# Queueing the HGRN scores and outputs between the k tiles of the projections, and the activation sums in four steps

## The chip, the core and the metric

The kernel runs on one core of one Trainium2 chip. TensorE multiplies matrices, VectorE and ScalarE do elementwise work (ScalarE also the functions: Sigmoid, Exp, Ln, Square), GpSimd (POOL) does small elementwise work and issues some DMAs, SyncE (SP) issues most of the weight DMAs. Each engine executes its own queue strictly in order; semaphores tie the queues together. The metric is the device time of one execution in microseconds (us). The kernel before takes 1414.12 us, the median of three runs (1412.45 to 1414.85).

## The reference: what is computed

One block of a network over 256 tokens of width 2048, all in float32. The projection `z = rms_norm(x) @ w_in` has eight parts, and two branches work on them:

```python
hq, hf, hi, hg, aq, ak, av, gates = jnp.split(z, SPLIT_POINTS, axis=-1)   # z = u @ w_in
g = lb + (1.0 - lb) * sigmoid(hf)          # forget gate;  log_g = log(g), kk = 1 - g
q = silu(hq) * HG_DK ** -0.5
o = hgrn2_scan(q, kk, hi, log_g)           # 8 heads of 128; S_t = diag(g_t) S_{t-1} + k_t v_t^T, o_t = S_t^T q_t
y_a = rms_norm(o, hg_norm_w) * silu(hg)
y_b = chunk_band_attention(aq, ak, av)     # 16 heads of 64, relative-position bias
merged = sigmoid(ga) * (y_a @ w_branch_a) + sigmoid(gb) * (y_b @ w_branch_b)
h = x + merged @ w_out
h = h + square(relu(rms_norm(h) @ w_up)) @ w_down
return rms_norm(h, norm_final_w)
```

The recurrence (HGRN) is what the change is about. It equals a masked product: `scores[t, s] = sum_k q[t, k] * exp(b[t, k] - b[s, k]) * kk[s, k]` for `s <= t`, where `b` is the running sum of `log_g`, and `o = scores @ v`. The factor depends on `t`, `s` and `k` together, so the kernel builds it from blocks of 2, 8, 32 and 128 tokens, within each of which the exponent splits into a factor for `q` and one for `kk`.

## The kernel before

**Products in three parts.** Every float32 product of a projection is made from a high and a low part of each operand. Two helpers load weights and make the parts: ScalarE casts the raw tile to the high part `wh_...` (line 89) and VectorE subtracts it from the raw tile for the low part `wl_...` (line 90). The raw tiles have six buffers, `wh` and `wl` four each; every such tile is 128 x 1024. This work is issued under a high priority, so that the scheduler puts it as early in each engine's order as the buffers permit. The activations `xT`, `ya`, `yb`, `mT`, `hT`, `uT` are kept transposed, also as high and low part.

**Two forms of a projection.** `gemm` (lines 154 to 158) makes 512 output columns for all 256 tokens: 16 k tiles, for each two halves `m` of the tokens, for each `mm3` with three products of 128x512 (lines 143 to 145), 96 products in all. `gemm_t` (lines 160 to 174) makes 256 transposed columns: for each of 16 k tiles and two column blocks one product of 128x512 and one of 128x256 (lines 170, 171), 64 products in all. Its two halves are added by `add_parts` (lines 178 and 179): ScalarE copies one half out of PSUM, VectorE adds the other. Both take one of the two buffers of the pool `ps_acc`; transposes take one of two in `ps_tp`, scores `ps` and outputs `po` one of two in `ps_sm`. A buffer is free when its last reader has read it.

**The order of the work.** Python emits the instructions in program order. A scheduler then orders them by priority, which follows program order outside the blocks of high priority, and a model of when each is ready; the result is one fixed queue for each engine. Nothing is chosen while it runs: an instruction that waits holds up all that stand behind it on its engine. ScalarE changes between the tables of its functions by a table load, which is an instruction of its own.

**The HGRN stage.** The eight heads are worked on as four pairs 0 to 3, in two groups of two pairs. `fq(u)` makes the inputs of a pair: the projections `hf` and `hq` (those of pairs 0 and 1 at the head of the kernel), then `hf_pair` (lines 298 to 310: `f`, `kk`, `lg` with an Ln, `b` by a scan) and `hq_pair` (lines 316 to 324: `sq` with a Sigmoid, then `q`). `v_chunk(g)` makes the values `v` of a group from `acc_hi`, `hg_chunk(g)` its output gate `gw` from `acc_hg`.

`hgrn_scores(n, ...)` (lines 348 to 425) makes the scores `sd` and `so` of a pair, all at once: first the diagonal and the tokens next to it (`ps{n}_1h`, line 355: 4 products of 128x192), then for each block size B of 2, 8 and 32 the factors (`el`, `kl`, `er`, `rr`, `qr`: VectorE differences and products, ScalarE Exp; lines 361 to 388) and the products `ps{n}_Bh` (line 395, 4 of 128x192), whose results VectorE writes into `sd` under masks, and last the block of 128 tokens (`c128`, `kc`, `ql`, lines 404 to 417, two products of 128x128, a copy to `so`). That makes 16 products of 128x192 and 2 of 128x128 for a pair. These products are plain float32, and the profile records each as two passes (its x8 are four products).

`hgrn_out(g, h0, ...)` (lines 428 to 461) makes the outputs of a pair for each half `m` of the tokens: `po` (lines 439 and 440; 4 + 2 products of 128x128), its squares `osq` on ScalarE (line 444), their sum `os` on VectorE, `rsqrt` (lines 95 and 96: VectorE `ms`, then a power `ro` on GpSimd) and `o` on VectorE (line 450). It returns a function that transposes `o` into `tpo` (line 458, two transposes for each `m`) and splits it into `ya` (ScalarE cast, VectorE subtraction). `hgrn_group` (line 476) calls this for both pairs of a group and then both of the transposing functions. The calls stand at lines 483 to 496:

```python
vs0 = v_chunk(0)
gws0 = hg_chunk(0)
s0 = hgrn_scores(0, *a0)
a2 = fq(2)
s1 = hgrn_scores(1, *a1)
a3 = fq(3)
hgrn_group(0, s0, s1, vs0, gws0)
```

and likewise for group 1, with the first attention projection `acc_q0` (`aq00`) before `hgrn_group(1, ...)`. The second one, `aq01`, is made in the attention stage, by `qk_chunk`, which reads `aq00` out with `add_parts` first. The next are `ak00` and `ak01`.

**After it.** The attention follows, then the gate projections, the merge (`ba`, `bb`), the output projection `wo` and the MLP (`up`, `dn`). The gates, `wo`, `up` and `dn` run as `Unit`s with a Strassen-like scheme on blocks of 2 x 2: seven products in place of eight, for which `combos` (lines 588 to 613) makes four sums S5, S4, S2 and S7 of blocks of the activations, each split into high and low part (a ScalarE cast, a VectorE subtraction of 128x512), from four block sums `a00` to `a11` (VectorE). The unit uses them in the order S5, S4, S2, S7. `combos` is called for `x` (before the gates), for the merged `m` (line 904, in the merge at `n == 2`), for `h` and for each quarter of `u`. `wo` runs as the units `wo0` and `wo2`, and the sums of `h` are made within `wo2`. For the last two it is the last entry of a unit's list of steps. A step carries a key, and `Unit.plain(n, ks)` issues, before its own products, all steps whose key is at most `ks[-1] // 4`, since these have to come before the k tile that it reads; `step` issues one step at each of the places between the unit's parts.

Of the kernel before, what the change touches and what calls it, by code (L numbers as in the profile page):

```python
# [16 lines left out]
P = 128  # L17
# [33 lines left out]
def tile_hybrid_block(  # L51
# [97 lines left out]

    def gemm(lhs, w, n0, nkt, what, wide=False):  # L150

        acc = new_acc(what)
        for kt, wh, wl in weights(w, n0, nkt, NC, what, wide=wide):
            for m in range(NM):
                mm3(acc[:, m, :], *lhs_of(lhs, kt, m), wh, wl, kt == 0, kt == nkt - 1)
        return acc

    def gemm_t(rhs, w, n0, nkt, what):

        acc = new_acc(what)  # L160
        for a in weights(w, n0, nkt, T, what):
            mm_t(acc, rhs, nkt, *a)
        return acc
# [184 lines left out]
    def hgrn_scores(n, kk, b, q):  # L348

        sd = hp.tile([P, 2, NM, P], F32, name=f"sd{n}", tag="sd", bufs=2)  # L350

        for h in range(2):
            ps = ps_sm.tile([P, NM, 192], F32, name=f"ps{n}_1{h}", tag="sm")
            for m in range(NM):
                nc.tensor.matmul(ps[:, m, :], kk[:, h, m * P:(m + 1) * P], q[:, h, m, :], start=True, stop=True)
            nc.vector.tensor_tensor(sd[:, h], ps[:, :, 0:P], bc(ident, 1, NM), op=ALU.mult)
            nc.vector.copy_predicated(sd[:, h].rearrange("p m (j u) -> p m j u", u=2)[:, :, :, 1],
                                      bc(mask1.bitcast(I32), 1, NM), ps[:, :, P:])

        for i, B in enumerate(LEVELS):  # L360
# [7 lines left out]
            kl = hp.tile([P, npar, 4, B], F32, name=f"kl{n}_{B}", tag="kl", bufs=3)  # L368
            nc.vector.tensor_tensor(kl, blocks(kk), el, op=ALU.mult)
# [7 lines left out]
            else:  # L377
# [4 lines left out]
                nc.vector.tensor_copy(rr, er[:, :, :, B - 1])  # L382
            qr = hp.tile([P, npar, 6, B], F32, name=f"qr{n}_{B}", tag="qr", bufs=2)
# [4 lines left out]
            nc.vector.tensor_tensor(qr[:, :, 5, :], qr[:, :, 4, :], bc(rr[:, :, 1], 2, B), op=ALU.mult)  # L388
            klf = kl.rearrange("p n v b -> p (n v b)")
# [14 lines left out]
        heads = lambda a: a.rearrange("p (h m) v b -> p h m v b", m=NM)  # L404
        r = rr.rearrange("p (h m) v -> p h m v", m=NM)
        r0, r1 = r[:, :, 0, :], r[:, :, 1, :]
        d128 = small.tile([P, 2, 4], F32, name=f"d128{n}", tag="d128", bufs=2)
        nc.vector.tensor_copy(c128[:, :, 2], r0[:, :, 3])
        nc.vector.tensor_tensor(c128[:, :, 1], r0[:, :, 2], r0[:, :, 3], op=ALU.mult)
        nc.vector.tensor_tensor(c128[:, :, 0], c128[:, :, 1], r0[:, :, 1], op=ALU.mult)  # L410
        nc.vector.tensor_copy(d128[:, :, 1], r1[:, :, 0])
        nc.vector.tensor_tensor(d128[:, :, 2], r1[:, :, 0], r1[:, :, 1], op=ALU.mult)
        nc.vector.tensor_tensor(d128[:, :, 3], d128[:, :, 2], r1[:, :, 2], op=ALU.mult)
        kc = hp.tile([P, 2, 4, 32], F32, name=f"kc{n}", tag="kc", bufs=1)
        nc.vector.tensor_tensor(kc, heads(kl)[:, :, 0], bc(c128, 3, 32), op=ALU.mult)
        ql = hp.tile([P, 2, 4, 32], F32, name=f"ql{n}", tag="ql", bufs=1)
        nc.vector.tensor_tensor(ql[:, :, 0, :], q[:, :, 1, 0:32], heads(er)[:, :, 1, 0, :], op=ALU.mult)
        nc.vector.tensor_tensor(ql[:, :, 1:4, :], heads(qr)[:, :, 1, 0:3, :], bc(d128[:, :, 1:4], 3, 32), op=ALU.mult)
# [461 lines left out]
    flush()  # L880


    mT = []

    def turned(lhs, n, name, src):

# [189 lines left out]
```

## Time and profile before

| | |
|---|---|
| median of three runs | 1414.12 us (1412.45 to 1414.85) |
| the profiled execution, its own time | 1415.3 us |
| its span | 1413.3 us |
| granted TensorE clock, mean | 0.996 |
| from the span's start to the first product of `acc_hi` | 54.9 us, TensorE busy 51.5 |
| HGRN stage, to the first product of `acc_ak` | 192.7 us, TensorE busy 187.5 |
| attention and first gates, 247.6 to 420 | 172.4 us, TensorE busy 172.3 |
| gates, merge and `wo`, 420 to 720 | 300.0 us, TensorE busy 296.9 |
| MLP, 720 to 1413.3 | 693.3 us, TensorE busy 682.0 |

In the rows of the profile, PE is TensorE, PEld its loading of weights, DVE VectorE, ACT ScalarE and POOL GpSimd; L143 is line 143 of the kernel. A group's row has line, engine, operation, result and operands, shape and count, then the busy time with the mean duration of one in ns, or least, mean and largest duration. A row of one instruction has its start and its duration in us. A row of a window of time has for each engine the busy time and, after x, the number of instructions, then the granted clock as a share of full speed, the DMA engines' busy share and the rate. A row of waits has the waiting instruction, an arrow to the instruction whose end released it, and the time that the engine stood idle, the number of such waits and the longest; the same arrow in square brackets behind a row gives the idle time ahead of that instruction. Products on TensorE overlap, and their ends are modelled, so that a duration is longer than the time from one start to the next.

### The profile page before, as it was taken

To read this page: it belongs to the slowest core of one execution; us is meant where nothing else is said; L and a number is where in the kernel's file an instruction comes from. 1 tells how busy PE (TensorE), PEld (TensorE's weight loads), DVE (VectorE), ACT (ScalarE), POOL (GpSimd) and SP (SyncE) were. 2 spreads that over 40 slices of the span, in tenths; PEclk is the share of its full clock that TensorE was granted. 3 is DMA by queue.
4 is the path that set the end of the run, shared out by engine and by line. 5 is a ranking of instruction groups with operands and counts; after the bars stand their busy time and mean duration, and the time that the engine had idled before them with its cause. 6 is when DMAs were issued, how large, how long until landed. Compare 5 with 4: busy or idle time off the path is not lost.

```text
span 1413.3 us, 18578 instructions
## 1 busy us (share of the span) xinstructions
PE 1390.2 (98%) x6562; PEld 1149.1 (81%) x6562; DVE 1120.0 (79%) x1410; ACT 912.6 (65%) x1173; POOL 138.6 (10%) x220
## 2 busy tenths in 40 slices
PE   9999999999999999999999999999999999999997
PEld 7888788878787888888877888888888888888885
DVE  7779887775658875687998878789777897878885
ACT  6766744464556665446767876677666876668764
POOL 3000101010000000001210001100101001110200
PEclk9999999999999999999999999999999999999999
DMA  9664444555568987558898899998899888998883
GB/s 318 234 195 148 135 158 135 184 173 167 183 223 256 263 235 256 185 177 258 249 282 252 245 269 243 278 280 245 259 292 283 254 229 250 289 293 263 258 255 115
DMA packets 122925, 327.42 MB, mean 232 GB/s; under 512 B 10944, under 2 KB 11712, under 8 KB 122448
## 3 DMA queue, kind: packets, MB, share of 16 engines
q1 hardware_dynamic: 103264, 264.80, 54.6%
q0 software_dynamic: 18416, 59.84, 21.3%
q10 hardware_dynamic: 1152, 1.60, 0.3%
q8 instruction: 51, 0.84, 0.2%
q14 instruction: 42, 0.34, 0.1%
HBM read 271.67 MB, written 10.49 MB: 200 GB/s over the span
## 4 chain that ended last, share of the span: by engine, by line
PE 89%; DVE 4%; DMA 2%; ACT 2%; issue 1%; POOL 0%; SPq 0%; POOLq 0%; ACTq 0%; DVEq 0%
PE acc_ak L171 2%; PE acc_aq L171 2%; PE acc_hf L171 1%; PE ps L395 1%; PE acc_hq L171 1%; PE tp_u L106 1%; PE acc_ga L144 1%; PE acc_ga L145 1%; PE acc_bb L143 1%; PE acc_ba L145 1%; PE acc_ga L143 1%; PE acc_av L143 1%; PE acc_bb L145 1%; PE acc_ba L143 1%; PE acc_ba L144 1%
## 5 line engine op out<-in xcount | busy, mean ns | idle before, releaser
L171 PE MATMUL acc_hf<-act_x,wh_hf 128*128 128x512 f32 x128 | 47.5, 408 | 1.7 <-DVE f L179 1.7
L171 PE MATMUL acc_aq<-act_x,wh_aq 128*128 128x512 f32 x128 | 47.8, 408 | 0.0
L171 PE MATMUL acc_hq<-act_x,wh_hq 128*128 128x512 f32 x128 | 45.9, 398 | 0.0
L171 PE MATMUL acc_ak<-act_x,wh_ak 128*128 128x512 f32 x128 | 44.8, 396 | 0.0
L170 PE MATMUL acc_aq<-act_x,wl_aq 128*128 128x256 f32 x120 | 35.2, 293 | 0.0
L90 DVE TENSOR_TENSOR wl_ga<-raw_ga,wh_ga 128x1024 fp32r<-128x1024 f32 x16 | 19.6, 1226 | 19.6 <-ACT wh_ga L89 19.6
L170 PE MATMUL acc_hf<-act_x,wl_hf 128*128 128x256 f32 x120 | 34.2, 285 | 0.0
L170 PE MATMUL acc_hq<-act_x,wl_hq 128*128 128x256 f32 x120 | 33.6, 280 | 0.0
L90 DVE TENSOR_TENSOR wl_av<-raw_av,wh_av 128x1024 fp32r<-128x1024 f32 x16 | 19.6, 1224 | 17.6 <-ACT wh_av L89 17.6
L170 PE MATMUL acc_ak<-act_x,wl_ak 128*128 128x256 f32 x120 | 33.5, 279 | 0.0
L89 ACT CAST wh_bb<-raw_bb 128x1024 fp32r<-128x1024 f32 x16 | 16.9, 1055 | 23.2 <-PE acc_ba L145 19.4
L90 DVE TENSOR_TENSOR wl_bb<-raw_bb,wh_bb 128x1024 fp32r<-128x1024 f32 x16 | 19.6, 1224 | 14.8 <-ACT wh_bb L89 14.8
L89 ACT CAST wh_av<-raw_av 128x1024 fp32r<-128x1024 f32 x16 | 16.9, 1053 | 22.0 <-PE acc_av L145 12.4
L89 ACT CAST wh_ba<-raw_ba 128x1024 fp32r<-128x1024 f32 x16 | 16.9, 1053 | 21.2 <-PE acc_bb L145 13.8
L89 ACT CAST wh_aq<-raw_aq 128x1024 fp32r<-128x1024 f32 x16 | 16.8, 1049 | 20.9 <-PE acc_aq L171 8.8
L90 DVE TENSOR_TENSOR wl_ba<-raw_ba,wh_ba 128x1024 fp32r<-128x1024 f32 x16 | 19.6, 1224 | 12.9 <-ACT wh_ba L89 12.9
L171 PEld LDWEIGHTS acc_hf<-act_x,wh_hf 128*128 128x128 f32 x128 | 24.2, 189 | 6.8 <-DVE f L179 2.0
L90 DVE TENSOR_TENSOR wl_aq<-raw_aq,wh_aq 128x1024 fp32r<-128x1024 f32 x16 | 19.6, 1224 | 12.5 <-ACT wh_aq L89 12.2
L171 PEld LDWEIGHTS acc_hq<-act_x,wh_hq 128*128 128x128 f32 x128 | 24.1, 188 | 5.6
L171 PEld LDWEIGHTS acc_aq<-act_x,wh_aq 128*128 128x128 f32 x128 | 24.2, 189 | 5.1 <-issue 0.7
L171 PEld LDWEIGHTS acc_ak<-act_x,wh_ak 128*128 128x128 f32 x128 | 23.9, 188 | 5.4
L89 ACT CAST wh_ga<-raw_ga 128x1024 fp32r<-128x1024 f32 x16 | 16.8, 1051 | 17.7 <-PE acc_ga L145 10.9
(1808 smaller groups left out, 5257.2 us busy)
## 6 DMA issues: line engine op xcount, KB each, us to landing
raw_hi<-in_w_in_n_dram SPq DMA_DIRECT2D x16, 512.0 KB, 4.2
raw_hg<-in_w_in_n_dram SPq DMA_DIRECT2D x16, 512.0 KB, 3.7
raw_aq<-in_w_in_t_dram SPq DMA_DIRECT2D x16, 512.0 KB, 4.3
raw_ak<-in_w_in_t_dram SPq DMA_DIRECT2D x16, 512.0 KB, 3.9
raw_av<-in_w_in_n_dram SPq DMA_DIRECT2D x16, 512.0 KB, 3.9
raw_ga<-in_w_in_t_dram SPq DMA_DIRECT2D x16, 512.0 KB, 4.6
raw_ba<-in_w_branch_a_dram SPq DMA_DIRECT2D x16, 512.0 KB, 4.5
raw_bb<-in_w_branch_b_dram SPq DMA_DIRECT2D x16, 512.0 KB, 4.6
```

Source lines behind the costliest of these rows:

```text
L89: (copy or nc.scalar.copy)(hi, src)
L90: nc.vector.tensor_tensor(lo, src, hi.bitcast(F32), op=ALU.subtract)
L106: nc.tensor.transpose(tp[:, j, :], src[:, j * P:(j + 1) * P], ident)
L143: nc.tensor.matmul(acc, hi, wh, start=first, stop=False, skip_group_check=True)
L144: nc.tensor.matmul(acc, hi, wl, start=False, stop=False, skip_group_check=True)
L145: nc.tensor.matmul(acc, lo, wh, start=False, stop=last, skip_group_check=True)
L170: nc.tensor.matmul(acc[:, cb, 0:T], wl[:, c], r[:, 0, :], start=False, stop=False)
L171: nc.tensor.matmul(acc[:, cb, :], wh[:, c], r.rearrange("p u t -> p (u t)"), start=kt == 0, stop=kt == nkt - 1)
L395: nc.tensor.matmul(ps[:, m, :], klf[:, a * P:(a + 1) * P], qrf[:, a * 192:(a + 1) * 192], start=True, stop=True)
```

## The change

A list `behind` holds pairs of a number and a function. `later` adds to its end; `tick(n)` subtracts n from the first number and, as long as the first number is at or below zero, takes the entry off and calls its function. `gemm` calls `tick(2)` ahead of the products of each k tile, `gemm_t` `tick(1)`. Numbers are not carried over: each entry counts from the moment at which it stands first.

`hgrn_scores` no longer emits its work but returns five steps: diagonal and factors of level 2; products of level 2 and factors of level 8; products of 8 and factors of 32; products of 32 and factors of 128; products of 128. Within the factors, `kl` now comes after `er` and `rr`, and `so` is allocated at the start. `scores(n, a, gap)` queues them with a number of 7 each (14 for the first of pair 0). `hgrn_out` returns two output steps and two transposing steps of a pair; `group` queues the four output steps of both pairs and then the four transposing steps, with a number of 4 each. The calls are reordered: the scores of pair 0 are queued ahead of `v_chunk(0)`, those of pair 1 ahead of `hg_chunk(0)`, the outputs of group 0 between `fq(2)` and `fq(3)`, the scores of pair 2 ahead of `v_chunk(1)`, of pair 3 ahead of `hg_chunk(1)`, the outputs of group 1 ahead of `aq00` and `aq01`, which are now both projected before the pool of the HGRN stage is closed. What is left in the queue then is emitted by `while behind: tick(9)`. `aq00` and `aq01` are read out by `add_parts` after that, in the attention stage.

`combos` returns four steps: all block sums and S5; the other three sums and the split of S4; the split of S2; the split of S7. For `x` all four run at once; for `m` two run at `bb` of `n == 2` and two at `bb` of `n == 3` (before: all at `ba` of `n == 2`); for `h` and `u` they are four entries of the unit's list of steps in place of one, with the same key. `Unit` is not changed.

```diff
+    behind = []
+
+    def tick(n):
+
+        if behind:
+            behind[0][0] -= n
+            while behind and behind[0][0] <= 0:
+                behind.pop(0)[1]()
+
+    def later(*steps):
+        behind.extend([n, f] for n, f in steps)
+
     def gemm(lhs, w, n0, nkt, what, wide=False):
 
         acc = new_acc(what)
         for kt, wh, wl in weights(w, n0, nkt, NC, what, wide=wide):
+            tick(2)
             for m in range(NM):
                 mm3(acc[:, m, :], *lhs_of(lhs, kt, m), wh, wl, kt == 0, kt == nkt - 1)
         return acc
...
         for a in weights(w, n0, nkt, T, what):
+            tick(1)
             mm_t(acc, rhs, nkt, *a)
         return acc
...
     def hgrn_scores(n, kk, b, q):
...
+        so = hp.tile([P, 2, P], F32, name=f"so{n}", tag="so", bufs=2)
+        held = {}
+
+        def diagonal():
+            for h in range(2):
...
+        def factors(i, B):
...
-            kl = hp.tile([P, npar, 4, B], F32, name=f"kl{n}_{B}", tag="kl", bufs=3)
-            nc.vector.tensor_tensor(kl, blocks(kk), el, op=ALU.mult)
...
                 nc.vector.tensor_copy(rr, er[:, :, :, B - 1])
+            kl = hp.tile([P, npar, 4, B], F32, name=f"kl{n}_{B}", tag="kl", bufs=3)
+            nc.vector.tensor_tensor(kl, blocks(kk), el, op=ALU.mult)
...
+            held[i] = kl, qr, er, rr
+
+        def level(i, B):
+            kl, qr, _, _ = held[i]
...
+        def factors128():
+            kl, qr, er, rr = held[2]
...
+            held["128"] = kc, ql
+
+        def level128():
+            kc, ql = held["128"]
...
+            nc.scalar.copy(so, ps)
+
+        f = [lambda i=i, B=B: factors(i, B) for i, B in enumerate(LEVELS)]
+        l = [lambda i=i, B=B: level(i, B) for i, B in enumerate(LEVELS)]
+
+        def both(*fs):
+            def go():
+                for x in fs:
+                    x()
+            return go
+
+        return (sd, so), [both(diagonal, f[0]), both(l[0], f[1]), both(l[1], f[2]), both(l[2], factors128), level128]
 
     ya = []
...
-        for m in range(NM):
+
+        def outputs(m):
...
-        def finish():
-            for m in range(NM):
-                tp = ps_tp.tile([P, 2, P], F32, name=f"tpo{n}{m}", tag="tp")
-                for h in range(2):
-                    nc.tensor.transpose(tp[:, h, :], os[m][:, h, :], ident)
-                split(hi[:, h0:h0 + 2, m * P:(m + 1) * P], lo[:, h0:h0 + 2, m * P:(m + 1) * P], tp)
-
-        return finish
+        def finish(m):
+            tp = ps_tp.tile([P, 2, P], F32, name=f"tpo{n}{m}", tag="tp")
+            for h in range(2):
+                nc.tensor.transpose(tp[:, h, :], os[m][:, h, :], ident)
+            split(hi[:, h0:h0 + 2, m * P:(m + 1) * P], lo[:, h0:h0 + 2, m * P:(m + 1) * P], tp)
+
+        return [lambda m=m: outputs(m) for m in range(NM)], [lambda m=m: finish(m) for m in range(NM)]
 
     def fq(u):
         if u == 0:
...
-    def hgrn_group(g, s0, s1, vs, gws):
-        f0 = hgrn_out(g, 0, s0, vs, gws)
-        f1 = hgrn_out(g, 2, s1, vs, gws)
-        f0()
-        f1()
+    def scores(n, a, gap, first=None):
+        sc, steps = hgrn_scores(n, *a)
+        later(*[(gap if i or first is None else first, f) for i, f in enumerate(steps)])
+        return sc
+
+    def group(g, s0, s1, vs, gws, gap):
+        o0, f0 = hgrn_out(g, 0, s0, vs, gws)
+        o1, f1 = hgrn_out(g, 2, s1, vs, gws)
+        later(*[(gap, f) for f in o0 + o1 + f0 + f1])
 
     ya += [new_act(f"ya{g}") for g in range(2)]
     a0, a1 = fq(0), fq(1)
+    s0 = scores(0, a0, 7, 14)
     vs0 = v_chunk(0)
+    s1 = scores(1, a1, 7)
     gws0 = hg_chunk(0)
-    s0 = hgrn_scores(0, *a0)
     a2 = fq(2)
-    s1 = hgrn_scores(1, *a1)
+    group(0, s0, s1, vs0, gws0, 4)
     a3 = fq(3)
-    hgrn_group(0, s0, s1, vs0, gws0)
+    s2 = scores(2, a2, 7)
     vs1 = v_chunk(1)
-    s2 = hgrn_scores(2, *a2)
+    s3 = scores(3, a3, 7)
     gws1 = hg_chunk(1)
-    s3 = hgrn_scores(3, *a3)
-    acc_q0 = gemm_t(xT, w_in_t, C_AQ, KD, "aq00")
-    hgrn_group(1, s2, s3, vs1, gws1)
+    group(1, s2, s3, vs1, gws1, 4)
+    acc_q = [gemm_t(xT, w_in_t, C_AQ + i * T, KD, f"aq0{i}") for i in range(2)]
+    while behind:
+        tick(9)
     hpool_cm.__exit__(None, None, None)
...
-        qT = [qk_chunk(C_AQ + g * NC + i * T, f"aq{g}{i}", rstd8_t, None if g or i else acc_q0) for i in range(2)]
+        qT = [qk_chunk(C_AQ + g * NC + i * T, f"aq{g}{i}", rstd8_t, None if g else acc_q[i]) for i in range(2)]
         kT = [qk_chunk(C_AK + g * NC + i * T, f"ak{g}{i}", rstd_t) for i in range(2)]
...
-    def combos(lhs, what, home, blocks=None):
+    def combos(lhs, what, home, made, blocks=None):
+
+        a = {}
+
+        def block(m, j):
+            if blocks:
+                a[m, j] = blocks[m, j]
+                return
+            a[m, j] = fours(token(f"a{m}{j}_{what}"))
+            x = lhs[j][:, :, :, m * P:(m + 1) * P].bitcast(F32)
+            nc.vector.tensor_tensor(a[m, j], x[:, :, 0, :], x[:, :, 1, :], op=ALU.add)
+
+        def final(i, s):
             t = home.tile([P, 4, 2, P], F32R, name=f"S{i}_{what}", tag=f"S{i}", bufs=1)
             split(t[:, :, 0, :], t[:, :, 1, :], s)
             made[i] = [[t[:, k, u, :] for u in range(2)] for k in range(4)]
-        return made
-
-    Sx = combos(xT, "x", tk)
+
+        def one():
+            for m in range(NM):
+                for j in range(2):
+                    block(m, j)
+            nc.vector.tensor_tensor(a[1, 1], a[1, 0], a[1, 1], op=ALU.subtract)
+            final(5, a[1, 1])
+
+        def two():
+            nc.vector.tensor_tensor(a[1, 0], a[0, 0], a[1, 0], op=ALU.subtract)
+            nc.vector.tensor_tensor(a[0, 0], a[1, 1], a[0, 0], op=ALU.subtract)
+            nc.vector.tensor_tensor(a[0, 1], a[0, 1], a[0, 0], op=ALU.add)
+            final(4, a[0, 1])
+
+        return [one, two, lambda: final(2, a[0, 0]), lambda: final(7, a[1, 0])]
+
+    Sx = {}
+    for f in combos(xT, "x", tk, Sx):
+        f()
...
                 for _, f in turned(mT, n - 1, f"m{n - 1}", ga):
                     f()
                 if n == 2:
-                    Sm = combos(mT, "m", tk)
+                    m_sums = combos(mT, "m", tk, Sm)
+            elif m_sums:
+                for f in m_sums[:2]:
+                    f()
+                del m_sums[:2]
         for m in range(NM):
             nc.vector.tensor_tensor(ga[n][m], ga[n][m], gb[n][m], op=ALU.add)
     m3 = ga[3]
...
-        last = factor if n0 else lambda: Sh.update(combos(hT, "h", sp))
-        return [(n, lambda n=n, m=m: one(n, m)) for n in (n0, n0 + 1) for m in range(NM)] + [(n0 + 1, last)]
+        return [(n, lambda n=n, m=m: one(n, m)) for n in (n0, n0 + 1) for m in range(NM)] + [
+            (n0 + 1, f) for f in ([factor] if n0 else combos(hT, "h", sp, Sh))]
...
-            def sums():
-                Su.update(combos(uT, f"u{qd}", tk, [blocks[m, j] for m in range(NM) for j in range(2)]))
-
-            return [(c, lambda c=c, m=m: one(c, m)) for c in (c0, c0 + 1) for m in range(NM)] + [(c0 + 1, sums)] * (not c0)
+            return [(c, lambda c=c, m=m: one(c, m)) for c in (c0, c0 + 1) for m in range(NM)] + [
+                (c0 + 1, f) for f in ([] if c0 else combos(uT, f"u{qd}", tk, Su, blocks))]
```

More of the change, by code (lines that the diff above doesn't have):

```diff
@@ L417, in hgrn_scores @@
-        nc.vector.tensor_tensor(ql[:, :, 0, :], q[:, :, 1, 0:32], heads(er)[:, :, 1, 0, :], op=ALU.mult)
-        nc.vector.tensor_tensor(ql[:, :, 1:4, :], heads(qr)[:, :, 1, 0:3, :], bc(d128[:, :, 1:4], 3, 32), op=ALU.mult)
-        ps = ps_sm.tile([P, 2, P], F32, name=f"ps{n}_128", tag="sm")
-        for h in range(2):
-            nc.tensor.matmul(ps[:, h, :], kc[:, h].rearrange("p v b -> p (v b)"),
-                             ql[:, h].rearrange("p v b -> p (v b)"), start=True, stop=True)
@@ L612, in combos @@
             made[i] = [[t[:, k, u, :] for u in range(2)] for k in range(4)]
-        return made
-    Sx = combos(xT, "x", tk)
+        def one():
+            for m in range(NM):
+                for j in range(2):
[11 more added lines that the diff above has]
+        f()
     ga, gb = [], []
@@ L880, in tile_hybrid_block @@
     flush()
-    mT = []
+    mT, Sm, m_sums = [], {}, []
     def turned(lhs, n, name, src):
```

68 lines of the change are left out of this document (24 added, 44 removed).

## The prediction

> **What bounds the kernel now.** I read the page's first part, then busy time by stage, TensorE's list of waits, and the rows of single stretches.
>
> ```profile
> span 1413.3 us, 18578 instructions
> PE 1390.2 (98%) x6562; PEld 1149.1 (81%) x6562; DVE 1120.0 (79%) x1410; ACT 912.6 (65%) x1173; POOL 138.6 (10%) x220
> ```
> ```profile
> core 0: us, PE busy (x) PEld busy (x) DVE busy (x) ACT busy (x) POOL busy (x), PEclk, DMA share, GB/s
> 54.90:98.40 43.50, 43.50 (x193) 36.04 (x192) 35.25 (x59) 33.78 (x42) 0.00 (x0) 1.00 0.60 197
> 98.40:155.60 57.20, 56.35 (x328) 50.15 (x327) 52.46 (x119) 38.29 (x47) 0.00 (x0) 1.00 0.45 146
> 155.60:213.90 58.30, 56.03 (x272) 45.97 (x270) 49.28 (x116) 32.63 (x49) 3.73 (x4) 1.00 0.45 148
> 213.90:247.60 33.70, 31.66 (x190) 27.46 (x189) 26.36 (x62) 13.46 (x21) 4.81 (x10) 1.00 0.43 135
> 247.60:283.00 35.40, 35.40 (x187) 30.28 (x186) 25.39 (x30) 17.24 (x20) 0.00 (x0) 1.00 0.59 185
> ```
> ```profile
> PE tpo L458 <- DVE o L450: 3.9, 7, 1.2
> PE acc_wo2c L143 <- ACT u_wo L707: 2.1, 1, 2.1
> PE acc_hf L171 <- DVE f L179: 1.7, 1, 1.7
> PE ps L395 <- DVE sd L357: 1.1, 3, 0.7
> PE acc_up00c L143 <- ACT act_h L89: 1.0, 1, 1.0
> PE acc_ga2c L144 <- DVE wl_ga2p11D L90: 1.0, 1, 1.0
> ```
> TensorE's own stream is the bound: it idles 23 us of 1413. An edit that keeps every matmul can only move waits. The HGRN stage, from the first product of `acc_hi` to the first of `acc_ak`, is 54.9 to 247.6: 192.7 us. TensorE idles 0.00 + 0.85 + 2.27 + 2.04 = 5.2 us of it, mostly at the transposes `tpo` behind `o`. VectorE is 92% busy from 98 to 156 us, so what it does late, TensorE feels.
>
> A wait costs more than its idle time, because a matmul's modelled end lies past the next one's start:
>
> ```profile
> L143 PE MATMUL acc_hi<-wh_hi,act_x x64: 387/389/483, 54.9 to 183.9; 128*128 128x512 f32 x64
> L171 PE MATMUL acc_ak<-act_x,wh_ak x128: 387/395/403, 247.6 to 348.5; 128*128 128x512 f32 x128
> 98.43 1.46 PE L355 MATMUL ps<-q,kk 128*128 128x192 f32 x8
> 237.28 0.39 PE L440 MATMUL po<-v,sd 128*128 128x128 f32 x2
> 270.02 0.39 PE L143 MATMUL acc_av<-wh_av,act_x 128*128 128x512 f32 x1
> 709.55 0.39 PE L144 MATMUL acc_wo2c<-wl_wo2p21B,S_m 128*128 128x512 f32 x1
> 709.77 0.39 PE L145 MATMUL acc_wo2c<-wh_wo2p21B,S_m 128*128 128x512 f32 x1
> 712.22 0.50 PE L143 MATMUL acc_wo2c<-wh_wo2r,act_m 128*128 128x512 f32 x1 [2.05 <-ACT u_wo L707]
> ```
> A product starts every 0.227 us and reads 0.39 long, so 0.16 us of each wait stands as busy. The stage's work: two `acc_ak` chunks take 247.6 to 270.0, 11.2 us each, so six such chunks (hf2, hq2, hf3, hq3 and two aq) 67.2; four chunks of 96 products 87.2; 128 passes of 128x192 at (1.46 - 0.16)/8 = 0.162, 20.7; 64 passes of 128x128 at 0.11, 7.0; 16 transposes at about 0.12 (estimated near these), 1.9. That is 184.0, so waits and changeovers cost 8.7 us.
>
> **The change, part by part.** No matmul, copy or DMA is added or dropped; the built order keeps each engine's instructions except three table loads of ScalarE fewer, at 1.28 us (row below). ScalarE is 39% to 78% busy in these stages, so I take 0; if its cover were gone, 3.9 us would be the most.
>
> *The waits that go.* Transposes now come a slot or more behind their `o`, and score bursts between k tiles: gain between the 5.2 idle and the 8.7 that hold changeovers too. The listed stops (7 at `tpo`, 3 at `ps`) at 0.16 make 6.8; I take 7.5, as fewer bursts also mean fewer changeovers.
>
> *Scores of pair 0 moved from behind `acc_hg` into `acc_hi`.* Before, their factors had 43 us of pure products as cover.
>
> ```profile
> 64.50 0.49 DVE L324 TENSOR_TENSOR q<-q,f 128x128 f32<-128x128 f32 x2
> 68.57 0.55 ACT L374 ACTIVATE er<-er 128x384 f32<-128x384 f32 x1
> 70.07 1.28 ACT L318 ACT_TABLE_LOAD   x1
> 71.36 0.63 ACT L318 ACTIVATE sq<-zq 128x512 f32<-128x512 f32 x1
> 72.03 0.69 DVE L321 SCALAR_TENSOR_TENSOR q<-zq,sq 128x512 f32<-128x512 f32 x1
> 74.25 0.32 ACT L376 ACTIVATE rr<-rr 128x128 f32<-128x128 f32 x1
> 75.12 0.29 DVE L388 TENSOR_TENSOR qr<-qr,rr 128x128 f32<-128x128 f32 x1
> ```
> The first burst `ps0_1` stands after 41 products: 54.9 + 41 x 0.227 = 64.2. Its `q` is half done at 64.8: wait 0.6. Level 2 stands 19 products and 8 passes later, at 64.8 + 4.3 + 1.3 = 70.4, and needs the last `qr0_2`. In VectorE's new order that is behind `q1`, which needs `sq1`. ScalarE's new order is `er0_2` (68.57), `rr0_2`, `rr0_8`, table load, `sq1`: 69.0 + 0.3 + 0.2, load to 70.8, `sq1` to 71.4; `q1` 0.6 and `qr` 0.3 more, 72.4. Wait 2.0. Level 8, level 32 and level 128 then find factors that I work out to end within 0.2 us of TensorE's arrival (VectorE has 12 us of queue for 12 us of products): 0.3 together, 0 to 1.5.
>
> *Outputs of group 0 in `hf3`.* `po020` reuses `po000`'s bank and waits for `o000`. On ScalarE, `osq000` now stands behind `zq2`, two casts, a table load, `lg2`, a third cast, a table load and `sq2`; from the end of `acc_hq2`, 7.0 us to `osq000`'s end, then `q2`, the reduction and `q2`'s halves 1.4.
>
> ```profile
> 233.09 0.17 DVE L95 TENSOR_SCALAR ms<-os 128x2 f32<-128x2 f32 x1
> 234.13 0.61 DVE L450 SCALAR_TENSOR_TENSOR o<-po,ro,gw 128x128 f32<-128x128 f32 x2 [0.88 <-POOL ro L96]
> ```
> From `ms` to the end of `o` is 1.65, so 10.1; TensorE comes 9.0 us after `acc_hq2`. Wait 1.1; by the same walk `po021` waits 0.4. Group 1 has no table loads there: 0.
>
> *The drain.* What is left in the queue at the end of `acc_aq01` is issued at once: all four transposes. This is the built order:
>
> ```
> TensorE: acc_aq01 (last 12), tpo100, tpo101, tpo120 [VectorE], tpo121 [VectorE], acc_ak00 [VectorE]
> ScalarE: osq121, wh_ak00_12 [TensorE], ya<-tpo100, ya<-tpo101, ya<-tpo120 [TensorE], aq00T<-acc_aq00, aq01T
> VectorE: o121, wl_ak00_12, ya<-tpo100, ya<-tpo101, ya<-tpo120, a00_x, aq00T<-acc_aq00, aq01T
> ```
> Both `ps_acc` buffers hold aq accumulators, so `acc_ak00` cannot start before VectorE has read `acc_aq00`; and there it stands behind the whole drain. `wh_ak00_12` takes the buffer of the last aq weights, so it starts when `acc_aq01` ends.
>
> ```profile
> 241.62 1.05 ACT L89 CAST wh_ak<-raw_ak 128x1024 fp32r<-128x1024 f32 x1 [0.56 <-PE acc_aq L171]
> 242.57 0.58 ACT L178 COPY aq00T<-acc_aq 128x512 f32<-128x512 f32 x1
> 243.05 0.38 ACT L89 CAST act_ya<-tpo 128x256 fp32r<-128x256 f32 x1
> 242.22 0.68 DVE L597 TENSOR_TENSOR a_x<-act_x 128x512 f32<-128x512 f32 x1
> 242.82 1.22 DVE L90 TENSOR_TENSOR wl_ak<-raw_ak,wh_ak 128x1024 fp32r<-128x1024 f32 x1
> 243.96 0.69 DVE L179 TENSOR_TENSOR aq00T<-acc_aq,aq00T 128x512 f32<-128x512 f32 x1
> 244.56 0.42 DVE L90 TENSOR_TENSOR act_ya<-tpo,act_ya 128x256 fp32r<-128x256 f32 x1
> ```
> From the end of `acc_aq01`: cast 1.05, `wl_ak` 1.14 (start to next start), `ya<-tpo100` 0.42 (frees a `ps_tp` bank), `tpo120` 0.45 with its weight load, ScalarE's `ya` 0.38, VectorE's `ya` 0.33, `a00_x` 0.60, `aq00T` 0.69 = 5.1, and some 0.2 of semaphores, less 0.4 of transposes that TensorE does meanwhile: wait 4.9 (4.0 to 5.5). Before, `aq00T` was read at 243.96, under `acc_aq01`, and TensorE did not stop at 247.6.
>
> *The clock.* The gap of 2.05 us in `wo2` is followed by this:
>
> ```profile
> 713.60:717.00 3.40, 3.40 (x10) 2.63 (x9) 3.07 (x4) 1.88 (x4) 0.00 (x0) 0.50 1.04 408
> ```
> For 3.4 us the granted clock is 0.50, which costs 1.7 us; the 1.7 us wait at `acc_hf` drew nothing. The drain's 4.9 us exceed both, and part of the slow spell falls into the wait itself: 1.5 (0 to 3.4). The 2.0 us at level 2 would read about 1.85 idle, between the two rows: I take 0, with 1.7 as its other end. The Trainium skill, page "TensorE: Matmul & The Clock Gate", section "Why this matters for your kernels", says that idle gaps over about 3 us bring half clock back; the trace has it after 2.05. By that page, level 2 is safe and the drain is not; the sum stays.
>
> *Sums in four steps.* In `wo2` the steps have keys 0 and 1, and `plain(1, (8, 9))` issues every step up to key 2 before its weights, so all four still come at once. The built order of all engines around `wo2` is unchanged: its 2.05 us and half clock stay, 0. In the `up` units one subtraction of `S5` moves ahead and one `S7` cast behind; in the merge an `S4` cast moves back. TensorE waited there nowhere (list above), 0; one 0.69 us operation late in each of five places bounds the loss at 3, the gain at 0.
>
> Sum: 0.6 + 2.0 + 0.3 + 1.1 + 0.4 + 4.9 + 1.5 - 7.5 = +3.3. The profiled execution took 1415.3 us (span 1413.3 and 2.0 around it), 1.2 above the median of the runs, 1414.12. On the median: 1417.4.
>
> **The rivals.**
> (a) Faster: the drain is covered. If `aq00T` is read before `acc_aq01` ends, 4.9 + 1.5 go, and the stage gains 7.5 - 4.4 = 3.1: 1411.0. It turns at one point, whether VectorE's `aq00T` runs ahead of the last `ya`. For it: before, it did. Against it: both orders are in-order queues, and `acc_ak00` names VectorE as its wait.
> (b) Slower still: the gap at level 2 draws half clock as the gap in `wo2` did (+1.7), and levels 8 to 128 miss by the 1.5 above (+1.2), each late VectorE row pushing the next: 1420.3. For it: 92% of VectorE before, and now no 43 us of cover. Against it: the 1.7 us wait that drew nothing.
> (c) No net change: waits move within the stage and the changeovers saved reach 8.7 while the slow spell falls wholly into the drain's wait: +0.6, 1414.7.
>
> **How the numbers follow.** Forecast 0.52, (b) 0.20, (c) 0.16, (a) 0.12. About 0.2%, 2.8 us, is what can be told from no change: below 1411.3 is faster, above 1416.9 slower. The forecast's own range, 1415.4 to 1420, lies three parts in five beyond 1416.9. Slower: 0.20 + 0.31 = 0.51; same: 0.16 + 0.21 = 0.37; faster: 0.12. The range reaches to (a) and past (b): 1411.0 to 1422.
>
> **What would show it.** Right: a TensorE wait of 4 to 5 us of `acc_ak` for VectorE's `aq00T` with clock 0.50 after it; about 2 us before the first `ps` of level 2, near 70 us; `tpo <- o` gone from the waits; `wo2`'s 2.05 us still there. Wrong: `acc_ak` starting at once, or waits at weights in the stage, which would mean that VectorE's queue has become the bound.

## The result, and the profile after

The changed kernel takes 1417.01 us, the median of 14 runs (1415.98 to 1419.26), beside 1414.20 us for the kernel before on the same chips (14 runs). The ratio is 1.002, with a 95% interval of 1.0012 to 1.0028: slower by 2.8 us. The forecast was 1417.4.

First the head of the page, then TensorE's list of waits (columns: the waiting instruction, what released it, idle us in total, times, longest).

```profile
span 1415.4 us, 18570 instructions
PE 1390.2 (98%) x6562; PEld 1150.4 (81%) x6562; DVE 1119.4 (79%) x1410; ACT 908.4 (64%) x1170; POOL 137.8 (10%) x220
```
```profile
PE tpo L494 <- DVE act_ya L90: 2.3, 1, 2.3
PE acc_wo2c L143 <- ACT u_wo L756: 2.1, 1, 2.1
PE ps L416 <- DVE qr L405: 1.9, 2, 1.7
PE acc_ak L185 <- DVE aq00T L193: 1.8, 1, 1.8
...
PE po L477 <- DVE o L487: 1.1, 1, 1.1
...
PE ps L372 <- DVE q L338: 0.5, 1, 0.5
...
PE po L476 <- DVE o L487: 0.2, 1, 0.2
```

The seven waits of `tpo` for `o` and the three of `ps` for `sd` are gone, and `acc_hf` no longer waits 1.7 us for `f` at the start of the kernel (which is not the change's doing, see below). In their place stand five waits in the HGRN stage and two at the handoff to `ak00`. The busy time of TensorE is the same to a tenth, though the stage is longer: what moved is waiting.

Where the time went shows in windows from the first product of `acc_hi` to that of `acc_ak`, and from there to that of `acc_av` (busy us and instructions of each engine, granted clock, DMA share, GB/s):

```profile
53.63:247.68 194.05, 186.37 (x978) 160.05 (x976) 163.67 (x353) 116.12 (x155) 7.96 (x12) 1.00 0.49 158
247.68:271.44 23.76, 23.76 (x128) 20.84 (x129) 18.38 (x24) 10.04 (x12) 0.29 (x2) 0.93 0.44 145
247.68:250.90 3.22, 3.22 (x10) 2.83 (x11) 3.22 (x7) 0.00 (x0) 0.29 (x2) 0.50 0.33 97
```

The stage takes 194.05 us in place of 192.72, 1.33 more. The two `ak` chunks, which the prediction's rows put at 247.6 to 270.0 before, 22.4, take 23.76, 1.36 more, with a clock of 0.50 for the first 3.2 us. Together that is +2.7, close to the 2.8 of the medians. The spans themselves differ by 2.1 only, because the profiled execution of the changed kernel reached `acc_hi` 1.3 us earlier (53.63 beside 54.9) and lost 0.7 behind `ak`. The early start is not the change: the instructions ahead of `acc_hi` are in the same order, and the run below that has the old HGRN code started at 53.22.

The handoff, in order of time (start, duration, idle before and what ended it):

```profile
243.50 1.23 DVE L90 TENSOR_TENSOR wl_ak<-raw_ak,wh_ak 128x1024 fp32r<-128x1024 f32 x1 [0.48 <-ACT wh_ak L89]
...
244.65 0.75 DVE L90 TENSOR_TENSOR act_ya<-tpo,act_ya 128x256 fp32r<-128x256 f32 x2
...
245.12 0.77 PE L494 MATMUL tpo<-ident,o 128*128 128x128 f32 x4 [2.29 <-DVE act_ya L90]
...
246.00 0.42 DVE L90 TENSOR_TENSOR act_ya<-tpo,act_ya 128x256 fp32r<-128x256 f32 x1 [0.60 <-ACT act_ya L89]
...
246.34 0.68 DVE L640 TENSOR_TENSOR a_x<-act_x 128x512 f32<-128x512 f32 x1
...
246.94 0.68 DVE L193 TENSOR_TENSOR aq00T<-acc_aq,aq00T 128x512 f32<-128x512 f32 x1
...
247.68 0.80 PE L185 MATMUL acc_ak<-act_x,wh_ak 128*128 128x512 f32 x1 [1.79 <-DVE aq00T L193]
```

Read down VectorE's rows: `wl_ak`, two splits of `ya`, a third, a sum of `x`, and only then the reading of `aq00T`, for which `acc_ak` waits. That is the drain as the built order had it. It costs two idle times of 2.29 and 1.79 us, since the transposes `tpo12` wait in the middle for a free bank.

And level 2 of pair 0:

```profile
68.16 1.28 ACT L332 ACT_TABLE_LOAD   x1
...
69.46 0.63 ACT L332 ACTIVATE sq<-zq 128x512 f32<-128x512 f32 x1
...
70.12 0.69 DVE L335 SCALAR_TENSOR_TENSOR q<-zq,sq 128x512 f32<-128x512 f32 x1 [1.09 <-ACT sq L332]
70.73 0.28 DVE L405 TENSOR_TENSOR qr<-qr,rr 128x128 f32<-128x128 f32 x1
...
71.16 1.54 PE L416 MATMUL ps<-qr,kl 128*128 128x192 f32 x8 [1.68 <-DVE qr L405]
```

VectorE stands idle for 1.09 us at pair 1's `q`, which waits for pair 1's Sigmoid and its table load; the last `qr` of pair 0 stands behind it, and TensorE behind that.

### The profile page after: what moved, and what is told of

Its sections match the earlier page's. It is cut to its first block, busy times and chain, and to the rows that moved or that the text cites. A ratio compares the mean times of both kernels' runs of the same rounds, so it can differ in the third digit from the quotient of the medians.

```text
span 1415.4 us, 18570 instructions
## 1 busy us (share of the span) xinstructions
PE 1390.2 (98%) x6562; PEld 1150.4 (81%) x6562; DVE 1119.4 (79%) x1410; ACT 908.4 (64%) x1170; POOL 137.8 (10%) x220
## 4 chain that ended last, share of the span: by engine, by line
PE 88%; DVE 4%; DMA 3%; issue 2%; ACT 2%; POOL 0%; POOLq 0%; SPq 0%; DVEq 0%; ACTq 0%
PE acc_ak L185 2%; PE acc_aq L185 2%; PE acc_hq L185 2%; PE acc_hf L185 2%; PE ps L416 1%; PE acc_aq L184 1%; PE acc_ga L144 1%; PE acc_ga L145 1%; PE acc_av L144 1%; PE acc_ga L143 1%; PE acc_ba L143 1%; PE acc_ba L145 1%; PE acc_av L145 1%; PE acc_av L143 1%; PE acc_ba L144 1%
## 5 line engine op out<-in xcount | busy, mean ns | idle before, releaser
L89 ACT CAST wh_ak<-raw_ak 128x1024 fp32r<-128x1024 f32 x16 | 16.8, 1050 | 22.7 <-PE acc_ak L185 11.5
L89 ACT CAST wh_hg<-raw_hg 128x1024 fp32r<-128x1024 f32 x16 | 16.8, 1050 | 20.8 <-PE acc_hg L145 12.6
```

Of the source, the lines that this page charges most:

```text
L89: (copy or nc.scalar.copy)(hi, src)
```

## The experiments

My theory: the loss is the handoff (VectorE reads `aq00` behind the drain, and the clock drops behind the gap) and the waits at the first burst, level 2 and `po`, less the old waits at `tpo`. The rivals: the four steps of the sums cost it; or VectorE is so full that a wait removed at one place comes back at another. All times are medians in us; ratios are to the kernel before, which ran beside them at 1413.7 to 1414.3, with 95% intervals. The changed kernel has the ratio 1.002 (1.0012 to 1.0028); where a run's interval overlaps that one, the windows of its profile decide and not its time.

### The two halves of the change alone

The first run takes `combos`, its callers and its step lists back to the form before; the second puts only those into the kernel before.

```diff
-    def combos(lhs, what, home, made, blocks=None):
+    def combos(lhs, what, home, blocks=None):
...
-            (n0 + 1, f) for f in ([factor] if n0 else combos(hT, "h", sp, Sh))]
+        last = factor if n0 else lambda: Sh.update(combos(hT, "h", sp))
```

> The change without its part on the sums: combos makes all four sums at once, as before. My theory (the loss of 2.8 us is the drain of the queue at the end of aq01 with the slow clock behind it, and the waits at level 2 and at po, less the old waits at tpo): same as the changed kernel, 2.0 to 3.5 us above the kernel before, that is 1416 to 1418. Rival (the sums in four steps cost it): within 0.7 us of the kernel before.

> The kernel before with the sums of activations in four steps and nothing else. My theory: no difference, within 1 us of the kernel before, and the wait of 2.05 us of acc_wo2c with the half clock behind it still there. Rival (the sums cost it): 2 to 3 us above the kernel before.

HGRN change alone: 1417.25 (1.0027; 1.0018 to 1.0036). Sums alone: 1414.39 (1.0005; 0.9996 to 1.0013), beside 1413.72 for the kernel before. The whole loss is in the HGRN part, and the sums in four steps make no difference that these runs can tell. In the second run the gap of `acc_wo2c` stands as it did, with the old waits at `tpo`, and the stage takes what it took before the change:

```profile
PE tpo L458 <- DVE o L450: 3.7, 6, 1.2
PE acc_wo2c L143 <- ACT u_wo L714: 2.1, 1, 2.1
```
```profile
53.22:245.88 192.66, 187.52 (x978) 159.64 (x977) 163.28 (x354) 118.14 (x156) 8.53 (x14) 1.00 0.48 156
245.88:268.28 22.40, 22.40 (x130) 19.54 (x129) 18.38 (x23) 11.57 (x14) 0.00 (x0) 1.00 0.57 187
```

### The handoff: an empty queue, or an early reading

Two ways to take the same waits away, one by the schedule and one by the buffer. The second cut leaves out how `aq` is scaled and how the new tile finds room, which the recorded text names.

```diff
-    s2 = scores(2, a2, 7)
+    s2 = scores(2, a2, 6)
...
-    s3 = scores(3, a3, 7)
+    s3 = scores(3, a3, 6)
```

> The changed kernel with the numbers of the scores of pairs 2 and 3 at 6 in place of 7, so that all eight steps of group 1 fit into aq00 and aq01 and nothing is left in the queue. My theory: the waits of 2.3 us at tpo12 and 1.8 us at acc_ak and the spell of clock 0.50 behind them go, 5.5 us less than the changed kernel: 1411 to 1412.5, 2 to 3 us below the kernel before. Rival (VectorE is too full, and what does not wait at the end waits inside the stage): the waits at tpo, po or at weights grow by as much, 1416 to 1418.

```diff
+    q00 = const.tile([P, 2, T], F32, name="aq00T")
...
-    acc_q = [gemm_t(xT, w_in_t, C_AQ + i * T, KD, f"aq0{i}") for i in range(2)]
+    acc_q = [gemm_t(xT, w_in_t, C_AQ, KD, "aq00")]
+    add_parts(q00, acc_q[0])
+    acc_q.append(gemm_t(xT, w_in_t, C_AQ + T, KD, "aq01"))
```

> The changed kernel with aq00 read out of PSUM into a tile of its own as soon as it is done, ahead of the outputs of group 1, so that its buffer is free before aq01 ends; in the built order the transposes tpo12 then stand behind the first k tile of ak00. The queue at the end is left as it is (the scaling of aq by rstd and by 0.125 is made in one instruction, for room in memory). My theory (the loss at the handoff is the order of VectorE's queue: ak00 waits for the reading of aq00 behind the drain): the waits of 2.3 and 1.8 us and the clock of 0.50 go, 5 us less than the changed kernel, 1411 to 1412.5. Rival (four transposes and their splits at once are too much for VectorE, whatever stands before ak00): tpo12 waits 2 us or more among the products of ak00, 1414 to 1416.

Empty queue: 1411.94 (0.9985; 0.9976 to 0.9994). Early reading: 1410.38 (0.9976; 0.9967 to 0.9986). Both take 5.1 us or more off the changed kernel's 1417.01 and both are faster than the kernel before. In the first, a wait of 0.6 us of `acc_ak` for `aq00T` is left. In the second the queue still holds all four transposes at the end; two stand ahead of `acc_ak` and two among its first products, and neither they nor `acc_ak` have a row in the list of waits, so the four transposes in the queue are not too much for VectorE once `acc_ak` no longer stands behind them. The loss was in the order: one read-out behind the drain. The 2.29 us at `tpo12` were no wait for that reading; they go because, with the buffer free, products of `ak00` stand ahead of `tpo12` and cover the splits of `ya`. The windows of the early reading, the stage and the two `ak` chunks:

```profile
53.47:242.42 188.95, 185.35 (x973) 159.63 (x972) 160.69 (x347) 113.38 (x150) 6.16 (x8) 1.00 0.47 157
242.42:265.60 23.18, 23.18 (x136) 20.09 (x135) 20.98 (x30) 12.69 (x18) 2.10 (x6) 1.00 0.62 194
```

The clock stays at 1.00. The `ak` chunks take 0.8 more than before the change; half of the drain's transposes now stand among them. Stage and chunks together are 212.13 us, 5.7 less than in the changed kernel; with the empty queue they are 212.34, 5.5 less.

### Level 2 of pair 0: later, or with nothing in between

Three edits. The whole pair two k tiles later; then only the products of level 2 later; then, from what these showed, pair 1's inputs behind `v_chunk(0)`.

```diff
-    s0 = scores(0, a0, 7, 14)
+    s0 = scores(0, a0, 7, 18)
```

> The changed kernel with the first number of pair 0 at 18 in place of 14, so that all its scores come two k tiles (2.7 us) later. My theory (level 2 waits 1.7 us and the diagonal 0.5 because the first burst comes too early, and the later levels have no slack to lose): the two waits go, 2.0 to 2.6 us less than the changed kernel, 1414.4 to 1415. Rival (VectorE's queue is the bound there: the wait moves to level 8, 32 or 128, or into group 0's outputs): 1416.5 to 1417.5, with other waits of ps or po of 1.5 to 2.5 us.

1418.13 (1.0029; 1.0017 to 1.0041). Neither came true. The first burst waits for nothing now, but level 2 waits longer and draws a clock near one half:

```profile
75.37 0.98 PE L416 MATMUL ps<-qr,kl 128*128 128x192 f32 x2 [2.83 <-DVE qr L405]
```
```profile
75.30:78.70 3.40, 3.33 (x10) 3.25 (x11) 2.87 (x6) 0.71 (x2) 0.00 (x0) 0.53 0.50 177
```

Factors and products are in the same step, so both moved; the factors then had still more of pair 1's work ahead of them, a Sigmoid with its table load before the last `rr`. "Too early" was the wrong reason.

```diff
-    def scores(n, a, gap, first=None):
+    def scores(n, a, gap, first=None, second=None):
...
+        gaps = [first or gap, second or gap] + [gap] * 3
+        later(*zip(gaps, steps))
...
-    s0 = scores(0, a0, 7, 14)
+    s0 = scores(0, a0, 7, 14, 11)
```

> The changed kernel with the number of pair 0's second step (level 2) at 11 in place of 7: the diagonal and the factors keep their place, the products of level 2 come two k tiles (2.7 us) later. Theory now, after the run with the whole pair later (the factors and not the products are bound, to the table loads of ScalarE and to sq1 and q1 of pair 1, which stand between them): the wait of 1.7 us at level 2 goes, that of 0.5 at the diagonal stays, 1415 to 1416. Rival (the factors of level 8 start with the products of level 2 and will be as late as these): 1.5 us or more of new waits at level 8 or 32, 1416.5 to 1417.5.

1416.91 (1.0025; 1.0014 to 1.0035). The rival came true: level 2 waits no more, and level 8, whose factors are emitted with the products of level 2, waits 1.60 us at 81.47.

```profile
81.47 0.73 PE L416 MATMUL ps<-qr,kl 128*128 128x192 f32 x3 [1.60 <-DVE qr L405]
```

```diff
-    a0, a1 = fq(0), fq(1)
+    a0 = fq(0)
     s0 = scores(0, a0, 7, 14)
     vs0 = v_chunk(0)
+    a1 = fq(1)
     s1 = scores(1, a1, 7)
```

> The changed kernel with the inputs of pair 1 (its f, q and their table loads) made after v_chunk(0) in place of before it, so that nothing of pair 1 stands between the factors of pair 0. Theory (the factors of pair 0 are late because ScalarE and VectorE do pair 1's Ln, scan, Sigmoid and q in between): the waits of 0.5 at the diagonal, 1.7 at level 2 and 0.2 go, 2.0 to 2.6 us less than the changed kernel, 1414.4 to 1415. Rival (VectorE has too much to do in these 40 us, in whatever order): the wait moves to a later level of pair 0 or 1, 1416.5 to 1418.

1414.86 (1.0005; 0.9995 to 1.0014), 2.2 below the changed kernel. No `ps` waits for `qr` any more, at any level of any pair, and the stage is 2.3 us shorter (191.79). It was not VectorE's load, which is the same (163.6 us), but what stood in its queue between pair 0's factors. At the first burst a wait of 0.2 for `q` is left. ScalarE also has one table load fewer from 55 to 90 us, six in place of seven; the run does not tell its share from that of the order.

### The outputs of group 0

```diff
-        later(*[(gap, f) for f in o0 + o1 + f0 + f1])
+        later(*zip([first or gap] + [gap] * 3 + [last or gap] * 4, o0 + o1 + f0 + f1))
...
-    group(0, s0, s1, vs0, gws0, 4)
+    group(0, s0, s1, vs0, gws0, 4, 8, 3)
```

> The changed kernel with the first output of group 0 at 8 in place of 4 and its transposes at 3, so that the outputs come four k tiles (2.8 us) later and the rest of the schedule is as it was. Theory (po020 waits 1.1 us for o000 because osq000 stands behind zq2, lg2, sq2 and their table loads on ScalarE, which end about 10 us after hq2): the waits of 1.1 and 0.2 at po go, 1.2 to 1.5 us less than the changed kernel, 1415.4 to 1415.8. Rival (the chain from po to o is longer than the two buffers of ps_sm allow at this spacing, at any place): the wait of 1.1 stays, 1416.5 to 1417.5.

1415.59 (1.0014; 1.0005 to 1.0023), 1.4 below the changed kernel. That time alone shows nothing: its interval overlaps that of the changed kernel, and a run below that changed neither the stage nor the gap in `wo2` came out as low (1415.65). The profile does: the wait of 1.1 us at `po` is gone, that of 0.16 has grown to 0.31, and the stage is 1.1 us shorter (192.91). That agrees with the reason given: by then pair 2's functions and their table loads on ScalarE are through. It does not agree with a chain that is too long at any place.

### The sums of h spread over wo2

In `wo2` the four steps come at once because of their keys. With a key of 99 they are taken one by one. First the blocks of `h` and the sums, alone and with the mended schedule (numbers 6 and 11 as above), then the sums alone.

```diff
-        return [(n, lambda n=n, m=m: one(n, m)) for n in (n0, n0 + 1) for m in range(NM)] + [
-            (n0 + 1, f) for f in ([factor] if n0 else combos(hT, "h", sp, Sh))]
+        return [(n if n0 else 99, lambda n=n, m=m: one(n, m)) for n in (n0, n0 + 1) for m in range(NM)] + [
+            (n0 + 1 if n0 else 99, f) for f in ([factor] if n0 else combos(hT, "h", sp, Sh))]
```

> The changed kernel with the keys of the steps of h in wo2 (the blocks and the four sums) set to 99, so that they are issued one by one between the parts of the unit and not all ahead of the first plain item. My theory (in wo2 the four steps change nothing because their keys make them come at once, and the gap of 2.05 us is ScalarE's copy u_wo behind a cast of the sums): the gap goes, and the spell of clock 0.50 behind it, 2.0 to 3.9 us less than the changed kernel, 1413 to 1415. Rival (the sums are then late for up0, which follows): a wait of 2 us or more at acc_up00 or acc_up0's use of S5, 1416 to 1418.

> The changed kernel with three edits at once: numbers of 6 for pairs 2 and 3 (no drain), 11 for level 2 of pair 0, keys of 99 for the steps of h in wo2. If the three are independent, 5.2 + 1.7 + 3.0 below the changed kernel: 1407 (1405.5 to 1409), 6 to 8 us below the kernel before. If the waits only move, 1410 to 1412.

1425.58 (1.0089; 1.0075 to 1.0103) and 1420.41 (1.0047; 1.0035 to 1.0060). Neither expected time held. The wait of `acc_wo2c` for `u_wo`, the gap of 2.05 us, is gone in both profiles, and so is the slow spell behind it, as the theory had it. But later, when `up0` has begun, a transpose of `h` waits 4.7 us, because the rows of `x` that are added to `wo2`'s result land late:

```profile
731.64 0.69 DVE L725 TENSOR_TENSOR h<-acc_wo2c,h 128x512 f32<-128x512 f32 x1 [5.12 <-DMA h<-in_x_dram]
...
732.48 0.87 PE L106 MATMUL tp_h<-ident,h 128*128 128x128 f32 x3 [4.70 <-DVE h L725]
```

These rows of `x` go into tiles of the same eleven buffers that hold the sums and block copies, so longer lives there are the likely reason; that they make the DMA late is argued from this, not measured apart. Behind that wait stand further ones, of `acc_wo2c` for `wl_wo2r` (1.4 us) and in `up0`, and the clock is 0.50 for 6.83 us from 732.21 and for 3.41 us from 742.45. From 695 to 760 us TensorE idles 9.2 us beside 3.5 in the changed kernel, and the slow clock costs up to 3.4 us more (less what of it falls into idle time); together that is about the loss of 8.6. The second run is the sum of the empty queue's gain and this loss: 1425.58 less 5.1 is 1420.5.

> The changed kernel with the keys of the four sums of h alone at 99; the blocks of h keep theirs, so they come as early as before and only the sums are issued one by one. After the run with all eight steps spread (x for up0's blocks came late, since the tiles of its sums were held longer): if the gap of 2.05 us in wo2 is made by the sums at once, it shrinks to under 1 us and the time falls by 1 to 4 us, 1413 to 1416; if tiles held longer are the cost, the blocks of h in up0 wait 2 us or more for h again, 1419 to 1425.

1415.65 (1.0015; 1.0006 to 1.0025). Undecided: the gap of 2.05 us stands unchanged. The built order kept S5's cast and the two copies `u_wo` in the same places on ScalarE, so this run did not move what it was meant to move, and its ratio overlaps that of the changed kernel. No wait of 2 us or more for `h` came back. Spreading all eight steps closes the gap in `wo2`; how to close it without the late rows of `x` stays open.

### The three mended places together

> The changed kernel with aq00 read early, pair 1's inputs after v_chunk(0) and group 0's outputs later, together. If the three terms add up: 1410.4 less 2.3 and 1.3, 1406.8 (1405.5 to 1408), 7 us below the kernel before. If only the handoff was real and the other waits move: 1409.5 to 1411.

The early reading of `aq00`, pair 1's inputs after `v_chunk(0)` and the later outputs of group 0: 1407.27 (0.9953; 0.9941 to 0.9966), 7.0 us below the kernel before and 9.7 below the changed one. The terms add up, and in the stage they do so to the hundredth: 188.95 us with the early reading, less 2.26 and 1.14 of the other two, is 185.55, and it takes 185.56. TensorE's idle time in the stage is down from 5.2 us before the change to 0.6:

```profile
53.43:238.99 185.56, 184.96 (x974) 159.66 (x972) 160.30 (x347) 112.11 (x149) 8.71 (x8) 1.00 0.50 160
```

## Why the prediction was right

Forecast 1417.4 against 1417.01, and the sum of its terms +3.3 against +2.7 in the trace. Each wait is its idle time (to the hundredth from the rows of the single products) and the 0.16 us that stand as busy:

| step | predicted | measured |
|---|---|---|
| first burst waits for `q` | 0.6 | 0.48 + 0.16 = 0.6 |
| level 2 waits for `qr` | 2.0 | 1.68 + 0.16 = 1.8 |
| levels 8 to 128 | 0.3 | 0.17 + 0.16 = 0.3 |
| `po020`, `po021` | 1.1, 0.4 | 1.11 + 0.16 = 1.3, 0.16 + 0.16 = 0.3 |
| drain | 4.9 | 2.29 + 1.79 + 2 x 0.16 = 4.4 |
| half clock behind it | 1.5 | 23.76 - 22.4 = 1.4 |
| old waits gone | -7.5 | 1.33 less the waits above = -7.5 |
| sums in four steps | 0 | 0.7 (-0.6 to 1.8) |

The gain of 7.5 is what remains when the waits above, 8.8, are taken from the stage's +1.33; the run with the early reading gives 7.4 in the same way (188.95, and the 0.8 by which the `ak` chunks are longer, less waits of 4.4, against 192.72). So the row "old waits gone" is a remainder and no reading of its own. The prediction had only the bounds 5.2 and 8.7 for it and chose 7.5 between them; that the choice agrees to a tenth is luck. So it is, in part, with the half clock behind the drain, chosen as 1.5 between 0 and 3.4: two other profiles with the same drain show 2.4 and 2.7 there.

- *The drain.* Both runs that take it away give 5.1 to 6.6 us back by their medians and 5.5 and 5.7 by their windows, against the 6.4 of the two terms and the 5.8 measured for them. What the prediction had as one wait is two, since the second pair of transposes stops TensorE first; their sum is 0.5 smaller than the walk through VectorE's rows.
- *Rival (a)* was the early reading, at 1411.0. Built, it gives 1410.38: its price was right and its condition was not met by the change as made.
- *Rival (b)* had level 2 drawing half clock. At 1.7 us of idle time it did not, as the prediction took it. With pair 0 later, at 2.83 us, it did.
- *Level 2.* The working named the cause, `qr` behind `q1` and `sq1` with its table load. I then argued in the experiments that the burst was merely too early; two runs refuted that, and the third confirmed the reason as first given.
- *`wo2`.* "Its 2.05 us and half clock stay": the gap stayed in each profile whose `wo2` was not changed, the half clock did not (last section).

## What to carry to other kernels

Here the queued work cost little where it stood between products, and most where it stood ahead of the reading of an accumulator whose buffer the next chunk needed: look at the handoff in the built order and ask which in-order engine reads the accumulator, and what stands ahead of that reading. When a burst waits for its factors, moving the burst moves the factors with it; first look for foreign work, table loads above all, between the factors in the queues. Reading one accumulator early was worth 6.6 us here by the medians, 5.7 by the windows, where the change as made lost 2.8.

## What the runs showed that was not expected

The gap of 2.05 us in `wo2` is followed by a spell of clock 0.50 in some executions and not in others, with the same instructions around it on TensorE. In the profiles that have the gap unchanged, eight show the spell (the kernel before and the changed one among them) and four do not. The 4.5 us from the end of the gap, in the changed kernel and in the run with the early reading:

```profile
713.92:718.42 4.50, 4.50 (x13) 3.51 (x14) 4.00 (x5) 2.98 (x4) 0.00 (x0) 0.63 1.04 414
```
```profile
707.91:712.41 4.50, 4.50 (x20) 3.69 (x21) 4.50 (x6) 4.24 (x6) 0.00 (x0) 1.00 1.03 407
```

Thirteen products in the one and twenty in the other: 1.6 us that come and go between executions. The drain's idle times of 2.29 and 1.79 us, 0.8 apart, drew a spell in all eight profiles that have them; single waits of 1.6 to 1.7 us drew none.

What decides is where a gap lies. Read in fine windows, the clock of the changed kernel is 0.50 from 247.46 to 250.87 and from 715.09 to 718.50: 3.41 us each time, with starts 467.63 us apart, which is 137 times 3.413. In all profiles that have spells between the head and the end of the kernel, these last 3.41 us or twice that, 6.83, and within one profile all edges lie whole multiples of 3.413 us apart, those of the rise at the head and of the fall at the end too. So the clock changes only at the edges of windows of that length, and the windows can be laid out in each profile. In the changed kernel one window holds the whole gap in `wo2`. With the early reading the edge at 707.37 us cuts the gap in two, 1.51 and 0.54 us of idle time:

```profile
711.67:715.09 3.42, 1.37 (x6) 0.98 (x6) 3.38 (x6) 3.27 (x5) 0.00 (x0) 1.00 1.04 413
715.09:718.50 3.41, 3.41 (x10) 2.62 (x9) 2.90 (x4) 1.81 (x3) 0.00 (x0) 0.50 1.03 410
```
```profile
703.96:707.37 3.41, 1.90 (x9) 1.24 (x7) 3.38 (x7) 1.56 (x3) 0.00 (x0) 1.00 1.03 410
707.37:710.79 3.42, 2.88 (x12) 2.36 (x13) 3.42 (x5) 3.42 (x6) 0.00 (x0) 1.00 1.03 414
```

In the eight profiles with the spell, one window has 1.91 to 2.06 us of the gap; in the four without, no window has more than 1.81. Over all windows at full clock, in all profiles, 1.91 us of idle time or more always brought half clock for the next one, and 1.68 or less never did; of those between, at 1.75 to 1.81, some did and some did not. The drain fills its window with 2.28 to 2.65, so it drew a spell in all eight, wherever their windows lay. Where the clock is already 0.50, less is enough: behind the drain of two runs (level 2 later, group 0 later) windows with 1.0 and 1.4 us of idle time brought a second slow one, and the two `ak` chunks took 25.12 and 24.79 us.

The Trainium skill, page "TensorE: Matmul & The Clock Gate", section "What's actually happening", says that the gate looks at windows of about 3.4 us that run freely, whatever the kernel does. The traces agree, with 3.413 us. The bound of about 3 us of idle time that the prediction cited from that page was too wide for this kernel, and the 2.05 us in `wo2` that it took as sure to bring half clock were not sure.

The table load ahead of `sq` took 1.30 us from its start to the start of `sq` (68.16 to 69.46). The Trainium skill, page "ScalarE: Activation LUTs", section "What ACT_TABLE_LOAD costs", gives 1283 ns for the load, which agrees, and about 1380 ns more for a drain with each switch, which does not show here.
